# Index queries of a decoder layer: split once where they are turned, kept as stacked high and low parts, and scored in even turns with the value projection

## The chip, the cores and the metric

The kernel runs on one core of a Trainium2 chip. The metric is the device time of one execution in microseconds, the median over several runs. The engines are TensorE (PE, and PEld for its weight loads), VectorE (DVE), ScalarE (ACT), GpSimd (POOL) and SyncE (SP). POOL and SP also issue DMA transfers.

## The reference

One layer of a hybrid decoder for 512 tokens of width 2048. What matters here is the sparse attention group, whose keys are chosen by an indexer of 16 heads of 64:

```python
def block(bargs):
    q_b, qi_b, wi_b, start = bargs
    qpos = start + jnp.arange(Q_BLOCK)
    dots = jnp.einsum('qhi,ki->qhk', qi_b, ki_s, ...) * (IDX_DIM ** -0.5)
    score = jnp.einsum('qh,qhk->qk', wi_b, jax.nn.relu(dots)) * (IDX_HEADS ** -0.5)
    visible = kpos[None, :] <= qpos[:, None]
    score = jnp.where(visible, score, -jnp.inf)
    _, idx = lax.top_k(score, topk)          # topk = 128
    k_sel, v_sel = k_s[idx], v_s[idx]
    logits = jnp.einsum('qhd,qkhd->qhk', q_b, k_sel, ...) * (dh ** -0.5)
    ...
```

`qi` and `ki` are projections of the normed tokens, turned by rotary angles (`rope`). Around it stand the norm and its conditioning by `c`, a stick-breaking attention group of 8 heads, the two gates, the output projection, and a gated MLP with a convolution. Everything is in float32.

## The kernel before

The layer is one program for the core, with tokens along the free dimension (tiles of 128 channels by 512 tokens). A float32 product is made of three matmuls over split operands: each operand is a high part (an ACT copy to the rounded type `fp32r`) and a low part (a DVE subtraction), and `mm3` (L177 to L179) adds high x high, high x low and low x high. Weights stream in on the SP queue as `raw` tiles and are split by `parts`: L167 on ACT writes `wh`, L169 on DVE writes `wl`, into three `rooms` that are used in turn. `split` (L196 and L198) does the same for activations.

The order on each engine is set when the program is built, by a scheduler that takes the code's order as a guide; an engine then runs its instructions strictly in that order. Code in `with behind(x)` is placed after `x`. Side work is written as Python generators, which the main code advances a step at a time.

**The units.** Most projections are done in 31 `unit` calls over `w_x`, each with seven block products on TensorE (a Strassen-like scheme). A unit calls `between` twice, and each call advances the generator `beside`. A part of `beside` is `index_ropes`: for each of eight tiles of index queries (two heads of 64 on 128 partitions) and one tile with the index key, it loads the tile `r` (tag `w`, two buffers), and `rope_steps` turns it: a DVE product (L746), four ACT copies that exchange halves (L749 and L750), then in the next step a DVE product (L752) and sum (L754). Its two temporaries lie in a tile with the tag `soft`, which has one buffer. The turned tile is saved by POOL to DRAM, `td_index[j]` (L786). Only tokens from 128 on (`LATE`, 384 of 512) are needed of the queries. POOL's queue in the units also has the saves of the units' results (`xd`, L882) and the accumulating saves of `mix` (L824).

**The indexer stage.** After the units, `indexer` loads the key and the eight query tiles (`queries`). For each head, `stacked` makes an operand of 128 partitions that holds the high part of the head's 64 channels on one half and their low part on the other (L944 on ACT, L945 on DVE). `score` multiplies it with the key's parts (L954), takes the relu (L956 on ACT, tag `w`) and accumulates with the head's weight on DVE (L959, L960). Scores are made for token blocks 1, 2 and 3 in turn, two heads of one block in a step, so 8 steps for each block. `seen` masks a finished block on POOL (L964), and `chosen` takes the 128 largest by rounds of MAX8 and MATCH_REPLACE8 on DVE (L971, L972); a few of these rounds are placed between the scores.

TensorE's other work in this stage is `values`, a projection (`w_vb`) of 192 matmuls that also is a generator; a step of it is six matmuls. After seven steps at the start, the loop alternates one step of `index` with steps of `fill`: two with each of the eight steps of block 1, and one with every second step after that. Then come the stick-breaking heads: POOL loads `xd` tiles (L892), ACT scales the query (L1055), TensorE makes `heads_z` (L1063), with the next part of the values (`values_narrow`, L1043) as its filling work.

Of the kernel before, what the change touches and what calls it, by code (L numbers as in the profile page):

```python
# [10 lines left out]
F32 = mybir.dt.float32  # L11
F32R = mybir.dt.float32r
BF16 = mybir.dt.bfloat16
I32 = mybir.dt.int32
AF = mybir.ActivationFunctionType
ALU = mybir.AluOpType
PSUM = bass.MemoryType.PSUM

P = 128
D = 2048  # L20
S = 512
# [55 lines left out]
def block_kernel(ctx: ExitStack, tc: tile.TileContext, A: dict, out: bass.AP):  # L77
# [14 lines left out]
    def slot(dt=F32):  # L92

        return t2k("F", SLOTS, dt)
# [99 lines left out]
    def split(src, hi=None, lo=None):  # L194
        hi = slot(F32R) if hi is None else hi
        pins["hi"] = act(hi, src, AF.Copy)  # L196
        lo = slot(F32R) if lo is None else lo
        tt(lo, src, hi.bitcast(F32), ALU.subtract)  # L198
        return hi, lo
# [149 lines left out]
    @contextmanager  # L349
    def behind(*pins):  # L350

        with ExitStack() as stack:
            for p in pins:
                stack.enter_context(tc.issue_after(p.ins))
            yield
# [401 lines left out]
        for _ in rope_steps(src, dst, cosv, sinv, half, n, t2k("ta", 2), t2k("sp", 2)):  # L757
            pass

    td_index = dram("index", 9)  # L760

    def index_ropes():

        tabs = [t2k("T", 2) for _ in range(2)]
        for i, t in enumerate(tabs):
            save(t, rope_d[1][:, i * S : (i + 1) * S])
        def get(j):
            r = t2k("w", 2)
            if j < 8:
                save(r[:, LATE], qid[j][:, LATE])  # L770
            else:
                save(r[:TN], td_tail[:TN])
            return r

        ahead = get(0)
        yield
        for j in range(9):
            r, ahead = ahead, get(j + 1) if j < 8 else None
            soft = sb.tile([P, 10 * P], F32, tag="soft", name=nm("soft"))
            tmp = soft[:, :S], soft[:, S : 2 * S]  # L780
            if j < 8:
                yield from rope_steps(r, [r], *tabs, 32, P, *tmp, LATE)
            else:
                yield from rope_steps(r, [r[:64], r[64:]], *tabs, 32, 64, *tmp)
            at = LATE if j < 8 else slice(0, S)
            save(td_index[j][:, at], r[:, at])  # L786
            yield

    def pause():
# [100 lines left out]
    def fetch(src, rows=slice(0, P)):  # L890
        t = slot()
        save(t[rows], src[rows])  # L892
        return t
# [23 lines left out]


    bias = [causal]

    def queries(j):
        t = slot()
        save(t[:, LATE], td_index[j][:, LATE])
        return t

    def indexer():

        kiR = split(fetch(td_index[8]))
        tail = fetch(td_tail, slice(0, TN))
        raw = [queries(j) for j in range(8)]  # L930
        yield
        wps = outs()
        for b in range(NQB):
# [3 lines left out]
        nc.vector.tensor_copy(wi.rearrange("p b h -> p (b h)"), wps[:, : NQB * IDXH])  # L937
        bias.extend(slot()[:, : (b + 1) * P] for b in range(1, NQB))
        yield

        def stacked(j, a):
            hi, lo = slice(a * IDXD, (a + 1) * IDXD), slice((1 - a) * IDXD, (2 - a) * IDXD)
            both = slot(F32R)
            pins["hi"] = act(both[hi, LATE], raw[j][hi, LATE], AF.Copy)  # L944
            pins["lo"] = tt(both[lo, LATE], raw[j][hi, LATE], both[hi, LATE].bitcast(F32), ALU.subtract)  # L945
            return both

        ops = []

        def score(n, b):  # L950
            W, sc = (b + 1) * P, bias[b]
# [23 lines left out]
            ts(sc, sc, TAKEN, NEG, ALU.not_equal, ALU.mult)  # L975

        for j in range(8):
            ops.extend(stacked(j, a) for a in range(2))
            for a in range(2):
                last = score(2 * j + a, 1)  # L980
            yield last
# [29 lines left out]
    for i in range(24):  # L1011
        run(index)
        if i < 8:
            h[2 * i] = split(halves_[i])
            if i < 6:
                halves_.append(fetch(hd_[i + 2]))
        with behind(pins["dots"], pins["hi"], pins["lo"]):
            run(fill, 2 if i < 8 else 1 - i % 2)
    run(fill, 2)


# [940 lines left out]
```

## Time and profile before

| | us |
|---|---|
| median of 3 runs | 2678.71 (2678.19 to 2680.88) |
| the profiled execution | 2679.04 |
| its span, first to last instruction | 2677.3 |
| TensorE busy | 2645.4 (99%) |
| DVE busy | 2372.4 (89%) |
| ACT busy | 1489.7 (56%) |
| POOL busy | 409.5 (15%) |

The granted TensorE clock is 0.998 over the span. The turns of index queries begin at 394 us and the last of their results is saved at 556 us; the indexer's scores run from 817 to 878 us.

How to read the rows: a timeline row has the start and the length in us, the engine, the line, the operation, what it writes <- what it reads, and in brackets the engine's idle time before it and what ended it. A row of a group has the count (x), the busy time in us, the mean in ns, and the idle time before. PE instructions overlap, so the distance between starts says what one costs. "L12" is line 12 of the kernel.

### The profile page before, as it was taken

To read this page: it belongs to the slowest core of one execution; us is meant where nothing else is said; L and a number is where in the kernel's file an instruction comes from. 1 tells how busy PE (TensorE), PEld (TensorE's weight loads), DVE (VectorE), ACT (ScalarE), POOL (GpSimd) and SP (SyncE) were. 2 spreads that over 40 slices of the span, in tenths; PEclk is the share of its full clock that TensorE was granted. 3 is DMA by queue.
4 is the path that set the end of the run, shared out by engine and by line. 5 is a ranking of instruction groups with operands and counts; after the bars stand their busy time and mean duration, and the time that the engine had idled before them with its cause. 6 is when DMAs were issued, how large, how long until landed. Compare 5 with 4: busy or idle time off the path is not lost.

```text
span 2677.3 us, 48400 instructions
## 1 busy us (share of the span) xinstructions
PE 2645.4 (99%) x18854; PEld 2440.7 (91%) x18854; DVE 2372.4 (89%) x3331; ACT 1489.7 (56%) x2143; POOL 409.5 (15%) x637
## 2 busy tenths in 40 slices
PE   8999999999999999999999999999999999999998
PEld 7779999999997888889999999999999998887876
DVE  9989989999987888889888999999999997888887
ACT  5445455655556776435565556555555555546443
POOL 0011112211122123332220000000000001003121
PEclk9999999999999999999999999999999999999999
DMA  9985768889894349866763457666666647559785
GB/s 362 340 293 186 230 217 241 239 256 275 263 265 162 108 142 327 283 196 201 227 201 104 134 182 192 182 180 181 183 179 182 179 134 244 154 173 243 217 228 158
DMA packets 182038, 564.84 MB, mean 211 GB/s; under 512 B 24868, under 2 KB 26676, under 8 KB 181808
## 3 DMA queue, kind: packets, MB, share of 16 engines
q1 hardware_dynamic: 120976, 399.59, 45.7%
q0 software_dynamic: 60336, 161.71, 23.3%
q8 instruction: 148, 2.42, 0.4%
q14 instruction: 82, 0.67, 0.1%
q10 hardware_dynamic: 496, 0.45, 0.1%
HBM read 451.96 MB, written 106.28 MB: 209 GB/s over the span
## 4 chain that ended last, share of the span: by engine, by line
PE 86%; DVE 4%; DMA 4%; issue 4%; ACT 2%; POOL 1%; ACTq 0%; SPq 0%; DVEq 0%; POOLq 0%
PE att L179 13%; PE att L178 13%; PE att L177 13%; PE acc L178 12%; PE acc L179 12%; PE acc L177 12%; PE att L1043 1%; DVE wl L169 1%; DMA raw<-in_w_qi 1%; DMA sumd<-F 1%; PE outs L178 1%; PE outs L177 1%; PE outs L1224 1%; PE outs L179 1%; PE outs L1111 1%
## 5 line engine op out<-in xcount | busy, mean ns | idle before, releaser
L167 ACT ACTIVATE wh<-raw 128x1024 fp32r<-128x1024 f32 (+2 forms) x783 | 821.6, 1055 | 887.7 <-DVE raw L294 186.5
L169 DVE TENSOR_TENSOR wl<-raw,wh 128x1024 fp32r<-128x1024 f32 (+2 forms) x783 | 944.2, 1213 | 122.8 <-ACT wh L167 116.2
L177 PE MATMUL acc<-F,wh 128*128 128x256 f32 (+3 forms) x2427 | 692.4, 286 | 1.2 <-ACT F L521 1.0
L179 PE MATMUL acc<-F,wl 128*128 128x256 f32 (+3 forms) x2427 | 690.2, 284 | 1.9 <-DVE wl L169 1.9
L178 PE MATMUL acc<-F,wh 128*128 128x256 f32 (+3 forms) x2427 | 689.9, 284 | 0.6 <-DVE F L198 0.3
L177 PE MATMUL att<-F,wh 128*128 128x256 f32 (+2 forms) x2420 | 689.7, 285 | 0.0
L179 PE MATMUL att<-F,wl 128*128 128x256 f32 (+2 forms) x2420 | 687.4, 284 | 0.5 <-DVE wl L169 0.5
L178 PE MATMUL att<-F,wh 128*128 128x256 f32 (+2 forms) x2420 | 686.8, 284 | 0.1
L177 PEld LDWEIGHTS acc<-F,wh 128*128 128x128 f32 (+1 forms) x2427 | 454.7, 187 | 12.8 <-ACT wh L167 3.0
L179 PEld LDWEIGHTS acc<-F,wl 128*128 128x128 f32 (+1 forms) x2427 | 454.9, 187 | 10.1 <-DVE wl L169 3.1
L178 PEld LDWEIGHTS acc<-F,wh 128*128 128x128 f32 (+1 forms) x2427 | 455.0, 187 | 8.7 <-DVE F L549 0.5
L177 PEld LDWEIGHTS att<-F,wh 128*128 128x128 f32 x2420 | 454.3, 188 | 7.6 <-ACT wh L167 1.7
L179 PEld LDWEIGHTS att<-F,wl 128*128 128x128 f32 x2420 | 454.2, 188 | 7.2 <-DVE wl L169 1.5
L178 PEld LDWEIGHTS att<-F,wh 128*128 128x128 f32 x2420 | 454.3, 188 | 6.6 <-DVE F L198 0.9
L178 PE MATMUL att<-wl,F 128*128 128x512 f32 x384 | 150.5, 392 | 0.6 <-DVE wl L169 0.6
L177 PE MATMUL att<-wh,F 128*128 128x512 f32 x384 | 150.3, 392 | 0.2 <-ACT wh L167 0.2
L179 PE MATMUL att<-wh,F 128*128 128x512 f32 x384 | 150.0, 391 | 0.0
L178 PE MATMUL acc<-wl,F 128*128 128x512 f32 x288 | 113.7, 395 | 2.1 <-DVE wl L169 2.0
L177 PE MATMUL acc<-wh,F 128*128 128x512 f32 x288 | 112.8, 393 | 1.4 <-ACT wh L167 1.4
L179 PE MATMUL acc<-wh,F 128*128 128x512 f32 x288 | 111.4, 391 | 0.0
L1423 POOL DMA_DIRECT2D yd<-w x41 | 22.8, 557 | 516.3 <-DVE w L1422 502.8
L332 DVE TENSOR_TENSOR raw<-raw,raw 128x1024 f32<-128x1024 f32 x79 | 96.4, 1220 | 1.3
(439 smaller groups left out, 4106.8 us busy)
## 6 DMA issues: line engine op xcount, KB each, us to landing
raw<-in_w_up SPq DMA_DIRECT2D x164, 512.0 KB, 3.8
raw<-in_w_x SPq DMA_DIRECT2D x128, 512.0 KB, 4.7
raw<-in_w_ada SPq DMA_DIRECT2D x124, 512.0 KB, 5.8
raw<-in_w_down SPq DMA_DIRECT2D x98, 512.0 KB, 4.7
xd<-F POOLq DMA_DIRECT2D x64, 256.0 KB, 4.2
mix<-F POOLq DMA_DIRECT2D x64, 256.0 KB, 6.6
F<-xd POOLq DMA_DIRECT2D x64, 256.0 KB, 5.6
raw<-in_w_o SPq DMA_DIRECT2D x32, 512.0 KB, 4.6
```

The costliest lines, as they stand in the source:

```text
L167: pins["wh"] = act(wh, raw, AF.Copy)
L169: pins["wl"] = tt(wl, raw, wh.bitcast(F32), ALU.subtract)
L177: mm(ps, ah, bh, start=first, stop=False, skip_group_check=not check)
L178: mm(ps, ah, bl, start=False, stop=False, skip_group_check=not check)
L179: return mm(ps, al, bh, start=False, stop=last, skip_group_check=not check)
L332: tt(a12, a12, s, ALU.subtract)
L1043: mm(narrow[b // 2][:, at], x, y, start=i == n == b % 2 == 0, stop=i == KT - 1 and n == 2, skip_group_check=True)
L1111: mm(o[:, kb * P :], vs[kb][:, hd % 4 * HD : (hd % 4 + 1) * HD], w[NQB - 1 - kb], start=i == 0, stop=i == 3, skip_group_check=True)
L1224: mm(o[:, b * P : (b + 1) * P], vs[kb][:, hd % 4 * HD : (hd % 4 + 1) * HD], pT[b][:, kb * P : (kb + 1) * P], start=kb == 0, stop=kb == b)
L1423: nc.gpsimd.dma_start(yd[j // 2][:, j % 2 * S : (j % 2 + 1) * S], a)
```

## The change

The index queries are split in `index_ropes`, right after they are turned: an ACT copy of the whole tile gives the high part and a DVE subtraction the low part, written over the two temporaries in `soft`. Four stores on POOL, each of 64 partitions, put them into DRAM tiles `stacked` of 128 x 512, one for each head, in the layout that `score` needs. The key keeps its store (`td_index`, now one tile). In the indexer `queries(n)` loads a ready operand for each head: eight at the start (`EARLY`), then two with each step of block 1. The sixteen ACT copies and sixteen DVE subtractions of the inner `stacked` are gone. `fill` gets one step with every step of the index loop, and is placed only behind the scores' matmul. The number of value steps is the same.

```diff
-    td_index = dram("index", 9)
+    td_index = dram("index", 1)[0]
+    stacked = [dr.tile([P, S], F32R, tag=f"stacked{n}", name=f"stacked{n}") for n in range(16)]
@@ index_ropes
-            at = LATE if j < 8 else slice(0, S)
-            save(td_index[j][:, at], r[:, at])
+            if j == 8:
+                save(td_index, r)
+            else:
+                hi, lo = (t[:, LATE].bitcast(F32R) for t in tmp)
+                act(hi, r[:, LATE], AF.Copy)
+                tt(lo, r[:, LATE], hi.bitcast(F32), ALU.subtract)
+                for a in range(2):
+                    own, other = slice(a * IDXD, (a + 1) * IDXD), slice((1 - a) * IDXD, (2 - a) * IDXD)
+                    save(stacked[2 * j + a][own, LATE], hi[own])
+                    save(stacked[2 * j + a][other, LATE], lo[own])
@@ the indexer
-    def queries(j):
-        t = slot()
-        save(t[:, LATE], td_index[j][:, LATE])
+    EARLY = 8
+
+    def queries(n):
+        t = slot(F32R)
+        save(t[:, LATE], stacked[n][:, LATE])
         return t
-        kiR = split(fetch(td_index[8]))
+        kiR = split(fetch(td_index))
-        raw = [queries(j) for j in range(8)]
+        ops = [queries(n) for n in range(EARLY)]
-        def stacked(j, a):
-            hi, lo = slice(a * IDXD, (a + 1) * IDXD), slice((1 - a) * IDXD, (2 - a) * IDXD)
-            both = slot(F32R)
-            pins["hi"] = act(both[hi, LATE], raw[j][hi, LATE], AF.Copy)
-            pins["lo"] = tt(both[lo, LATE], raw[j][hi, LATE], both[hi, LATE].bitcast(F32), ALU.subtract)
-            return both
-
-        ops = []
         for j in range(8):
-            ops.extend(stacked(j, a) for a in range(2))
+            ops.extend(queries(n) for n in range(len(ops), min(2 * j + EARLY + 2, 16)))
@@ the loop over index and fill
-        with behind(pins["dots"], pins["hi"], pins["lo"]):
-            run(fill, 2 if i < 8 else 1 - i % 2)
+        with behind(pins["dots"]):
+            run(fill)
```

Three places show how instructions move. The first is DVE at the end of one unit, where a query has been turned and the next is begun. Before (L298 adds a unit's sum, L594 is a step of the conditioning, L280 a sum of weights, L746 begins the next query's turn):

```order
L169 TENSOR_TENSOR wl_69<-raw_4224,wh_66 128x1024
L298 TENSOR_TENSOR sp_4325<-att_4222,ta_4258 128x256
L746 TENSOR_TENSOR soft_4358<-w_4122,T_4058 128x384
L594 SCALAR_TENSOR_TENSOR raw_4289,macc_67<-raw_4289,raw_94 128x1024
L169 TENSOR_TENSOR wl_75<-raw_4230,wh_72 128x1024
L280 TENSOR_TENSOR raw_4494<-raw_4460,raw_4462 128x1024
L169 TENSOR_TENSOR wl_82<-raw_4228,wh_78 128x1024
L752 TENSOR_TENSOR soft_4358<-soft_4358,T_4059 128x384
```

Now (L791 is the new subtraction):

```order
L791 TENSOR_TENSOR soft_4132<-w_4070,soft_4132 128x384
L298 TENSOR_TENSOR sp_4338<-att_4230,ta_4266 128x256
L594 SCALAR_TENSOR_TENSOR raw_4297,macc_67<-raw_4297,raw_94 128x1024
L169 TENSOR_TENSOR wl_75<-raw_4238,wh_72 128x1024
L280 TENSOR_TENSOR raw_4507<-raw_4473,raw_4475 128x1024
L746 TENSOR_TENSOR soft_4371<-w_4130,T_4066 128x384
L169 TENSOR_TENSOR wl_82<-raw_4236,wh_78 128x1024
L752 TENSOR_TENSOR soft_4371<-soft_4371,T_4067 128x384
```

The subtraction of the query turned before stands ahead of L298, and the next query's L746 has moved from behind L298 to behind L280, ahead of a weight split.

The second is POOL between two such queries. Before (L786 saves a turned query, L770 loads the one after next):

```order
L824 DMA mix_1916<-F_4296 128x512
L786 DMA index_1906<-w_4122 128x384
L882 DMA xd_1640<-F_4353 128x512
L770 DMA w_4590<-qid_885 128x384
L882 DMA xd_1641<-F_4354 128x512
L824 DMA mix_1917<-F_4366 128x512
```

Now (L794 and L795 are the new stores of high and low parts; L833, L891 and L771 are the former L824, L882 and L770):

```order
L833 DMA mix_1924<-F_4309 128x512
L891 DMA xd_1640<-F_4366 128x512
L891 DMA xd_1641<-F_4367 128x512
L794 DMA stacked_1908<-soft_4371 64x384
L794 DMA stacked_1909<-soft_4371 64x384
L795 DMA stacked_1908<-soft_4371 64x384
L795 DMA stacked_1909<-soft_4371 64x384
L833 DMA mix_1925<-F_4379 128x512
L771 DMA w_4608<-qid_885 128x384
```

One store has become four, and they stand behind both saves of the unit and ahead of a `mix` save and the next query's load.

The third is POOL at the end of the indexer. Before (L964 masks blocks 1, 2 and 3 as their scores are complete; L892 loads the first heads):

```order
L964 AFFINE_SELECT F_9218<-F_9218 128x128
L964 AFFINE_SELECT F_9219<-F_9219 128x128
L892 DMA F_9826<-xd_1618 128x512
L892 DMA F_9828<-xd_1619 128x512
L892 DMA F_9843<-vd_898 128x512
L892 DMA F_9845<-vd_899 128x512
L892 DMA F_9847<-vd_900 128x512
L892 DMA F_9849<-vd_901 128x512
L892 DMA F_9875<-xd_1620 128x512
L892 DMA F_9877<-xd_1621 128x512
L964 AFFINE_SELECT F_9220<-F_9220 128x128
```

Now:

```order
L965 AFFINE_SELECT F_9266<-F_9266 128x128
L965 AFFINE_SELECT F_9267<-F_9267 128x128
L965 AFFINE_SELECT F_9268<-F_9268 128x128
L901 DMA F_9842<-xd_1618 128x512
L901 DMA F_9844<-xd_1619 128x512
L901 DMA F_9859<-vd_898 128x512
```

The loads of the first heads have moved behind the mask of block 3. On TensorE, 30 matmuls of L1043 now stand ahead of the first `heads_z`, where there were 38.

## The prediction

> **What bounds the kernel now.** I read the page first: busy shares and the chain.
>
> ```profile
> PE 2645.4 (99%) x18854; PEld 2440.7 (91%) x18854; DVE 2372.4 (89%) x3331; ACT 1489.7 (56%) x2143; POOL 409.5 (15%) x637
> PE 86%; DVE 4%; DMA 4%; issue 4%; ACT 2%; POOL 1%; ACTq 0%; SPq 0%; DVEq 0%; POOLq 0%
> ```
>
> TensorE sets the time nearly everywhere, so an edit matters only where it makes TensorE wait or stop waiting. DVE, at 89%, has little air. The change touches two stages, so next I read the stretches: one unit of the projections, in which an index query is turned, and the three parts of the indexer stage.
>
> ```profile
> 413.05:432.09 19.04, 19.04 (x170) 19.04 (x169) 17.33 (x21) 11.57 (x17) 3.96 (x7) 1.00 0.84 244
> 817.30:847.50 30.20, 27.98 (x130) 23.04 (x130) 26.24 (x44) 21.78 (x43) 2.58 (x5) 0.94 0.41 141
> 847.50:864.00 16.50, 15.42 (x68) 11.64 (x68) 14.03 (x36) 9.18 (x18) 0.29 (x1) 1.00 0.21 65
> 864.00:878.30 14.30, 12.98 (x53) 9.24 (x52) 13.19 (x30) 9.32 (x16) 4.73 (x9) 1.00 0.52 184
> ```
>
> Columns are the length, busy PE, PEld, DVE, ACT, POOL, then clock, DMA share and GB/s. The unit is full on TensorE and 17.33 of 19.04 us full on DVE. In the indexer the first part (scores of block 1) contains a TensorE stall at a lower clock, and in the other two DVE is 14.03 of 16.50 and 13.19 of 14.30 us busy while TensorE waits in small pieces.
>
> **Part 1, the indexer: what it gains.** TensorE's rows there:
>
> ```profile
> 820.45 0.39 PE L179 MATMUL att<-wh,F 128*128 128x512 f32 x1
> 822.97 1.09 PE L954 MATMUL acc<-F,F 128*128 128x256 f32 x4 [2.13 <-DVE F L945]
> 823.89 0.41 PE L177 MATMUL att<-wh,F 128*128 128x512 f32 x1
> 828.24 0.64 PE L954 MATMUL acc<-F,F 128*128 128x256 f32 x4
> ...
> 844.34 0.64 PE L954 MATMUL acc<-F,F 128*128 128x256 f32 x4
> 844.81 0.40 PE L177 MATMUL att<-wh,F 128*128 128x512 f32 x1
> 847.56 0.87 PE L954 MATMUL acc<-F,F 128*128 128x384 f32 x4
> 848.27 0.40 PE L177 MATMUL att<-wh,F 128*128 128x512 f32 x1
> ...
> 872.76 1.07 PE L954 MATMUL acc<-F,F 128*128 128x512 f32 x4
> 873.66 0.39 PE L177 MATMUL att<-wh,F 128*128 128x512 f32 x1
> ```
>
> By starts, four score matmuls (L954) take 0.47, 0.71 and 0.90 us for blocks 1, 2 and 3, and twelve value matmuls (two steps) take 2.75 us (844.81 to 847.56), so one step takes 1.375 us. The stall of 2.13 us waits for the split of the stacked queries (L945), and the twelve value matmuls behind it take 4.35 us (823.89 to 828.24), 1.6 more than at full clock. What is removed, and what DVE has beside it:
>
> ```profile
> L945 DVE TENSOR_TENSOR F<-F,F 64x384 fp32r<-64x384 f32 x16 | 8.8, 553 | 4.3 <-ACT F L944 3.8
> L944 ACT ACTIVATE F<-F 64x384 fp32r<-64x384 f32 x16 | 8.3, 517 | 2.9 <-DMA F<-index 2.7
> ACT w L956 <- DVE F L960: 10.0, 22, 1.1
> L960 DVE SCALAR_TENSOR_TENSOR F<-w,wi,F 128x256 f32<-128x256 f32 x15 | 7.2, 483 | 1.4 <-ACT w L956 0.9
> L198 DVE TENSOR_TENSOR F<-F,F 128x512 fp32r<-128x512 f32 x8 | 5.5, 690 | 1.0 <-ACT F L196 0.8
> ```
>
> The first two rows are what goes; the last two are DVE's other work in block 1. The third row is from the waits of 847.5 to 878.4: there the score's relu waits for DVE's accumulation (L960) 22 times, and TensorE for the relu. The even turns put eight value steps (11.0 us of TensorE) out of block 1 and into blocks 2 and 3, where DVE was the pace. TensorE's bare work from the first score to the first matmul of the next values (817.33 to 878.33, 61.0 us): 8 x (0.47 + 0.71 + 0.90) = 16.6, and 150 value matmuls at 0.229 = 34.4, so 51.0; the slack is 10.0. With the new order the parts need 8 x (0.47 + 1.375) = 14.8, then 16.7, 18.2 and a last step of 1.4 on TensorE. DVE needs some 15 of 14.8 in block 1 (16 accumulations at 0.48, eight splits at 0.69 less overlap, two or three weight splits at 1.22), about 15.2 of 16.7 and 17.4 of 18.2 in the others (its busy time there, with one more weight split each and the accumulations that now end after 878.3). TensorE leads, narrowly. I leave 1.5 us of the slack standing for block 1, where loads of `hd` now queue among eight more loads on POOL: **gain 8.5**. Its ends: 10.0 if no wait is left, 3.7 if only the stall and its slow clock go.
>
> A price stands at its end. POOL asks for the first heads only behind the third mask (`seen`), which waits for DVE's last accumulation:
>
> ```profile
> 864.17 0.47 POOL L964 TENSOR_SCALAR_AFFINE_SELECT F<-F 128x128 f32<-128x128 f32 x1 [16.27 <-DVE F L960]
> 864.66 1.09 POOL L892 DMA_DIRECT2D F<-xd  x2
> F<-xd POOLq DMA_DIRECT2D x6, 256.0 KB, 3.1
> 878.33 0.28 PE L1043 MATMUL att<-wh,F 128*128 128x256 f32 x1
> 882.77 0.81 PE L1063 MATMUL acc<-F,F 128*128 128x384 f32 x2
> ```
>
> From the last accumulation, mask and two issues take about 1.1 us and landing 3.1: 4.2. TensorE has, behind its last score, 2.75 us of values and 30 of the 38 matmuls that now take 4.45 us (3.5): 6.25, less 1.4 for the relu and accumulation, so 4.85 against 4.2. Hidden, with 0.65 to spare; beyond it each us is lost. The eight postponed matmuls are only moved.
>
> **Part 2, the units: what it costs.** Each turned query (eight of them, one a unit) gains an ACT copy of 128x384 and a DVE subtraction, and on POOL four half-height stores for one. The DVE subtraction is about 0.55 us (as L754 below) and lies where DVE idles 0.46 us for L298; it costs nothing by itself. ACT is 11.57 of 19.04 busy. POOL gets 24 more stores here and 8 more loads in the indexer at 0.54 us, and is 3.96 of 19.04 busy. But both halves lie in `soft`, which has one buffer: the next query's turn (L746 on DVE, L749 and L750 on ACT) must wait until all four stores have landed. Before, `soft` was free as soon as L754 had read it. One unit, DVE then ACT:
>
> ```profile
> 411.36 1.23 DVE L169 TENSOR_TENSOR wl<-raw,wh 128x1024 fp32r<-128x1024 f32 x1 [0.23 <-ACT wh L167]
> 413.05 0.42 DVE L298 TENSOR_TENSOR sp<-att,ta 128x256 f32<-128x256 f32 x1 [0.46 <-PE att L179]
> ...
> 417.27 1.22 DVE L169 TENSOR_TENSOR wl<-raw,wh 128x1024 fp32r<-128x1024 f32 x1
> 419.21 0.56 DVE L752 TENSOR_TENSOR soft<-soft,T 128x384 f32<-128x384 f32 x1 [0.72 <-ACT soft L750]
> 420.02 0.55 DVE L754 TENSOR_TENSOR w<-soft 128x384 f32<-128x384 f32 x1
> 420.92 1.22 DVE L169 TENSOR_TENSOR wl<-raw,wh 128x1024 fp32r<-128x1024 f32 x1
> ...
> 430.40 1.23 DVE L169 TENSOR_TENSOR wl<-raw,wh 128x1024 fp32r<-128x1024 f32 x1 [0.24 <-ACT wh L167]
> 415.71 1.06 ACT L167 ACTIVATE wh<-raw 128x1024 fp32r<-128x1024 f32 x1 [1.66 <-PE att L178]
> 417.05 0.53 ACT L749 ACTIVATE soft<-w 32x384 f32<-32x384 f32 x1
> 419.21 0.72 ACT L823 ACTIVATE F<-F,c_col 128x512 f32<-128x512 f32 x1
> ```
>
> The subtraction comes at 412.5, after the first L169 here. Then 0.55, a hop of 0.1 to POOL and one issue of 0.55 until the fourth store is issued at 413.7. The price of landing is the unknown. Nearest rows, from the DMA list of 400 to 540 us:
>
> ```profile
> index<-w POOLq DMA_DIRECT2D x8, 192.0 KB, 5.5
> xd<-F POOLq DMA_DIRECT2D x15, 256.0 KB, 4.2
> DMA to landing us min/median/max: 4.7/5.4/6.8
> ```
>
> The last row is of `index` alone. I take T = 5.5, the store that these replace, from the same place in the program: each is half its size, but four go together with a DMA share of 0.84. Bounds 4.2 and 6.8. So `soft` is free at 419.2; ACT's four turns, which began at 417.05 and took 2.16, now begin there; L752 starts at 421.4 instead of 419.21; and in order behind it L330, L754, L331 and the weight split of 420.92, which now ends at 424.3 instead of 422.14. Who waits: the split rooms are three deep, a room came free at 415.7, and TensorE's products take 19.04 / 7 = 2.72, so the product that needs this split starts at 423.8, its low part at 424.05. The slack is 1.9 us: the first time TensorE loses 0.3.
>
> It repeats. From L752 (419.21) to the subtraction behind the last L169 (430.40) DVE has 12.3 us, 11.87 without two small gaps. So the loop from one subtraction to the next is 1.2 + T + 2.16 + 11.87 = 15.2 + T, 20.7 at 5.5 against 19.04 of TensorE: 1.7 us later in each unit. Eight turns wait, the last (the key, two copies for four) shorter by about 0.7: in all 2.16 + 7 x 1.7 - 0.7 - 1.9 = **loss 11.4**. At T = 4.2 it is about 1, at 6.8 about 22; under 3.8 nothing. Beyond the slack every 0.1 us of T is 0.8 us of time.
>
> The Trainium skill (DMA: Bandwidth & Descriptors, Anatomy of one DMA) puts a DMA of this path at 2.0 us plus its bytes at 436 GB/s: an estimate by that page is 2.2 us for a store of 96 KB, under which DVE would not wait and the sum would be 2670.5, rival (b). The trace disagrees: 192 KB would be 2.5 by it, and took 5.5. The same page (Rules for kernel authors) says that two transfers to disjoint partition halves serialize and are better as one; this speaks against the four stores, and no run here shows a half-height one.
>
> **The sum.** The profiled execution took 2679.04 with a span of 2677.3, 0.3 above the median of the runs. 2679.0 - 8.5 + 11.4 = **2682**.
>
> **The rivals.** (a) The stores land late: T of 6 to 6.8, the longest of `index`, makes DVE's wait cost 15 to 22, so 2686 to 2692. For it: DMA is shared with the weight loads at 0.84. Against: 96 KB is less than 192. It is slower beyond 0.2% (5.4 us) from T = 5.8. Chance 0.27. (b) The stores hide: T at 3.8 or less leaves the gain alone, 2670.5, and up to 4.4 the loss is 3 and the change still measurably faster. For it: 256 KB of `xd` in 4.2 in the same stretch. Against: `index` never under 4.7. Chance 0.18. (The 2.0 us and bytes of the Trainium skill, DMA: Bandwidth & Descriptors, Anatomy of one DMA, would give this case.) (c) The even turns don't bring what they say: DVE keeps the pace of blocks 2 and 3, or the heads' loads come later than 4.85 us and TensorE stands before L1063; the gain is the stall's 3.7, less up to 2 there: 2679 + 11.4 - 2.7 = 2688. For it: DVE's 17.4 of 18.2. Chance 0.08. (d) The forecast, within 0.2% (about what a measurement of this kernel can tell from no change) of 2679, at 2682: 0.47.
>
> So faster 0.18, same 0.47, slower 0.27 + 0.08 = 0.35. The forecast's own range is 2674 to 2684. The full one reaches to the gain with a loss of 2 (2672) and to (a) at T = 6.6 (20 - 8.5, 2690).
>
> **What would show it.** In the new profile: no L944 or L945 group, no stall before the second pair of scores and the clock at 1.00 there (part 1); the first matmul of the next values about 8.5 us sooner after the first score; POOL's heads loads behind the mask and no idle before the heads' first matmul. In the units: idle before L746 on DVE and the first L749 on ACT put down to the stores of `stacked`, some 2 us each; units of about 20.7 instead of 19.04 us while queries are turned; TensorE idle before L179 by DVE's `wl`. If units stay at 19.04 us, T or my slack is wrong; if the indexer's stretch does not shrink, the even turns are.

## The result and the profile after

The changed kernel takes 2694.6 us (median of six runs) against 2679.8 of the kernel before in the same session: a ratio of 1.0056, 95% interval 1.0042 to 1.0070, so slower by 11 to 19 us. The prediction was 2682, in a range of 2672 to 2690. The profiled execution took 2695.74 us with a span of 2694.0, against 2679.04 and 2677.3.

The busy times on the page of the changed kernel say little, as they did before; the first row is the engines, the second the chain of what ended last:

```profile
PE 2647.7 (98%) x18854; PEld 2446.4 (91%) x18854; DVE 2366.4 (88%) x3323; ACT 1482.6 (55%) x2135; POOL 426.8 (16%) x669
PE 77%; issue 8%; DMA 6%; DVE 4%; POOL 2%; ACT 2%; ACTq 0%; POOLq 0%; SPq 0%; DVEq 0%
```

TensorE has the same work (2647.7 for 2645.4 us), but its share of the chain is 77% for 86%, and DMA's is 6% for 4%. What it waits for stands in the waits of 390 to 590 us, in which eight queries and the key are turned (engine, line, tile, releaser: sum, times, longest):

```profile
DVE soft L746 <- DMA stacked<-soft: 19.1, 7, 3.4
ACT soft L749 <- DMA stacked<-soft: 17.9, 7, 3.1
```

Seven times both engines stand 2.0 to 3.4 us at the head of a turn until the stores of the turn before it have landed (an eighth wait, 2.8 us at the key, has another releaser's name). The first such unit in the timeline, across engines:

```profile
413.40 0.52 ACT L790 ACTIVATE soft<-w 128x384 fp32r<-128x384 f32 x1
414.21 1.10 POOL L794 DMA_DIRECT2D stacked<-soft  x2 [5.31 <-ACT soft L790]
414.42 0.55 DVE L791 TENSOR_TENSOR soft<-w,soft 128x384 fp32r<-128x384 f32 x1
415.30 1.07 POOL L795 DMA_DIRECT2D stacked<-soft  x2
420.93 0.56 DVE L746 TENSOR_TENSOR soft<-w,T 128x384 f32<-128x384 f32 x1 [2.13 <-DMA stacked<-soft]
423.14 0.56 DVE L752 TENSOR_TENSOR soft<-soft,T 128x384 f32<-128x384 f32 x1 [0.51 <-ACT soft L750]
423.62 0.42 DVE L330 TENSOR_TENSOR sp<-att,ta 128x256 f32<-128x256 f32 x1
424.18 0.36 PE L177 MATMUL att<-F,wh 128*128 128x256 f32 x1 [1.10 <-DVE sp L330]
```

POOL issues the four stores one after the other until 416.4; `soft` comes free at 420.9; the turn's L752 follows at 423.1, and behind it L330, the addition that reads the accumulator `r2`. TensorE's last product of the unit, T4, adds into that accumulator and so waits for L330: 1.10 us idle here, and 1.2 to 2.3 us in each of the next seven units. The lengths of the units from one subtraction L791 to the next (first, fifth and seventh of seven; length, busy PE, PEld, DVE, ACT, POOL, then clock, DMA share, GB/s):

```profile
414.42:434.84 20.42, 19.32 (x171) 19.16 (x170) 17.70 (x24) 11.78 (x18) 5.65 (x10) 1.00 0.82 234
497.45:519.00 21.55, 19.30 (x171) 19.14 (x170) 17.68 (x24) 11.74 (x18) 5.62 (x10) 1.00 0.78 223
539.86:562.81 22.95, 20.78 (x168) 20.61 (x168) 17.89 (x23) 12.89 (x19) 5.42 (x10) 0.93 0.75 211
```

No unit has its 19.04 us; DVE's busy time has hardly moved (17.7 for 17.33), it is idle time that was added. In the last of them TensorE also ran at a lower clock after its wait. In the indexer the two other parts stand, from the first score to the first matmul of the next values:

```profile
836.76:852.66 15.90, 15.22 (x82) 12.96 (x81) 12.54 (x24) 10.50 (x24) 6.95 (x13) 1.00 0.97 319
852.66:869.66 17.00, 16.97 (x81) 14.54 (x80) 15.76 (x37) 9.96 (x19) 0.29 (x1) 1.00 0.27 88
869.66:889.17 19.51, 19.51 (x87) 15.98 (x86) 18.52 (x41) 12.30 (x21) 0.47 (x1) 1.00 0.18 55
```

That is 52.4 us for 61.0, with TensorE busy in 51.7 of them and its clock at 1.00. Right behind it the heads wait:

```profile
885.54 1.07 PE L955 MATMUL acc<-F,F 128*128 128x512 f32 x4
889.17 0.36 PE L1044 MATMUL att<-wh,F 128*128 128x256 f32 x1
889.21 0.74 DVE L961 SCALAR_TENSOR_TENSOR F<-w,wi,F 128x512 f32<-128x512 f32 x1
890.02 0.29 POOL L965 TENSOR_SCALAR_AFFINE_SELECT F<-F 128x128 f32<-128x128 f32 x1 [18.01 <-DVE F L961]
890.50 1.09 POOL L901 DMA_DIRECT2D F<-xd  x2 [0.18 <-issue]
891.57 2.12 POOL L901 DMA_DIRECT2D F<-vd  x4
893.39 0.63 ACT L1056 ACTIVATE F<-F 128x512 f32<-128x512 f32 x1 [1.59 <-DMA F<-xd]
893.68 2.13 POOL L901 DMA_DIRECT2D F<-xd  x4
894.11 0.89 PE L1064 MATMUL acc<-F,F 128*128 128x384 f32 x2 [1.17 <-ACT F L1056]
901.10 0.88 PE L1064 MATMUL att<-F,F 128*128 128x384 f32 x2 [1.45 <-DMA F<-xd]
```

The last accumulation ends at 889.95, the mask follows, and only then POOL asks for the first head, the values and the second head. Both heads stand for their loads. In the kernel before, all eight loads stood behind the second mask, at 864.17, and the third came 17 us after it:

```profile
865.74 2.12 POOL L892 DMA_DIRECT2D F<-vd  x4
867.85 1.07 POOL L892 DMA_DIRECT2D F<-xd  x2
881.45 0.29 POOL L964 TENSOR_SCALAR_AFFINE_SELECT F<-F 128x128 f32<-128x128 f32 x1 [12.53 <-DVE F L960]
```

**Where the time went.** How much later the same matmul starts than before, taken along the program: 1.9 us ahead of the first turn, 18.7 behind the last, 19.4 at the first score, 10.8 at the next values, 13.8 at the second head, 16.7 at the end. So: units +16.8, indexer -8.6, heads +2.95, stretch between units and indexer +0.7; together +11.8. The other 4.9 lie in stages whose instructions are the same. Some 1.5 us of them came at about 160 us and as much at about 2620, each beside a granted clock below 1 (0.75 from 160 to 165 us, 0.83 from 2615 to 2625) that the kernel before did not have there. Such stages vary from one profile to the next: the first turn (L746) starts between 393.7 and 397.1 us in the profiles of this study, with the same work ahead of it.

### The profile page after: what moved, and what is told of

Read it like the earlier page. It is cut to its first block, busy times and chain, and to the rows that moved or that the text cites. A ratio compares the mean times of both kernels' runs of the same rounds, so it can differ in the third digit from the quotient of the medians.

```text
span 2694.0 us, 48470 instructions
## 1 busy us (share of the span) xinstructions
PE 2647.7 (98%) x18854; PEld 2446.4 (91%) x18854; DVE 2366.4 (88%) x3323; ACT 1482.6 (55%) x2135; POOL 426.8 (16%) x669
## 4 chain that ended last, share of the span: by engine, by line
PE 77%; issue 8%; DMA 6%; DVE 4%; POOL 2%; ACT 2%; ACTq 0%; POOLq 0%; SPq 0%; DVEq 0%
PE acc L178 12%; PE acc L179 12%; PE acc L177 12%; PE att L177 11%; PE att L179 11%; PE att L178 11%; DVE wl L169 1%; DMA raw<-in_w_qi 1%; PE outs L178 1%; PE outs L177 1%; PE outs L179 1%; PE att L1044 1%; DMA T<-in_w_va 1%; DMA mix<-F 1%; DMA F<-x1d 0%
## 5 line engine op out<-in xcount | busy, mean ns | idle before, releaser
L179 PEld LDWEIGHTS acc<-F,wl 128*128 128x128 f32 (+1 forms) x2427 | 455.0, 187 | 10.1 <-DVE wl L169 3.1
```

Source lines behind the costliest of these rows:

```text
L179: return mm(ps, al, bh, start=False, stop=last, skip_group_check=not check)
```

## The experiments

The theory from the comparison: the stores hold `soft`, so the next turn waits for their landing, and a loop runs through DVE (subtraction, four issues, landing, turns, the rest of DVE's unit) that is longer than TensorE's unit. The heads lose part of the indexer's gain because the even turns moved their loads behind the third mask. Rivals: the added work itself; the turns or the split alone as the source of the gain; a wait that only T4's position causes.

**1. Room of its own.** The four stores stay; what they read is no longer needed by the next turn.

```
+        soft = sb.tile([P, 10 * P], F32, tag="soft", ...)     # once, ahead of the turns
-            soft = sb.tile([P, 10 * P], F32, tag="soft", ...) # in each turn
-            tmp = soft[:, :S], soft[:, S : 2 * S]
+            tmp = soft[:, :S], soft[:, S - P : 2 * S - P]
-                hi, lo = (t[:, LATE].bitcast(F32R) for t in tmp)
+                hi, lo = soft[:, 7 * P :].bitcast(F32R), r[:, LATE].bitcast(F32R)
```

> The change, but the stores no longer hold the room that the next query's turn needs: `soft` is taken once for all turns, the high part has columns of its own in it, and the low part is written over the turned query, which is not stored any more. The same four half-height stores, the same copy and subtraction, the same loads, the same indexer. Theory (the turn waits for the stores of the turn before it, and TensorE's last product of a unit, T4, waits behind that turn for the addition L330): no idle before L746, no TensorE idle before T4, units of 19.04 us again while queries are turned; the 16.8 us that the units lost are back and the time is 2674 (2679.8 - 8.6 + 2.95, the stages of the indexer and the heads) to 2678 (2694.6 - 16.8). Rival (the added work itself, 24 more stores on POOL and one more instruction each on ACT and DVE per query): the units stay above 20 us and the time above 2690.

Measured: 2676.7 us, ratio to before 0.9985 (0.9976 to 0.9994). A unit, and the wait that took the place of DVE's:

```profile
414.00:433.04 19.04, 19.04 (x170) 19.04 (x169) 17.80 (x23) 11.98 (x17) 5.61 (x10) 1.00 0.90 253
```

```profile
POOL w L771 <- DMA stacked<-w: 24.0, 6, 4.7
```

The units are back at 19.04 us with the same ACT copy, DVE subtraction and 32 stores in them, and TensorE is never idle there. The landing is no shorter; POOL now waits for it, six times 4 us, before it loads the query after next, and no wait of TensorE or DVE in these units is put down to POOL or to these stores. The added work is ruled out: the wait on the room was the loss. This version is faster than both kernels.

**2. The split with the old turns, and the even turns without the split.** Two halves of the change:

```
 # split_only: the change, but
-            run(fill)
+            run(fill, 2 if i < 8 else 1 - i % 2)
 # turns_only: the kernel before, but
-            run(fill, 2 if i < 8 else 1 - i % 2)
+            run(fill)
```

> The change with the old turns of the first values: two value steps for each of the first eight index steps, then one for every second. So the split is in the units, and the indexer has no split, but its old order. Before, 61.0 us lie between the first score and the first matmul of the next values, in the changed kernel 52.4. Theory (part of the gain is the stall on the split and the slow clock behind it, 3.7; the rest is the even turns, for DVE sets the pace of blocks 2 and 3 in the old order): 57.3 us there, units as in the changed kernel, heads' loads not waited for; in all 2679.8 + 16.8 - 3.7 = 2693 to 2696. Rival (the split was the whole of it: DVE without the 8.8 us of L945 no longer sets the pace in either order): 52.4 to 53 us there, 2688 to 2691. Second rival (the even turns are the whole of it): 61 us there, 2697.

> The kernel before, with the even turns alone: one value step behind each index step; the queries are still loaded whole and split in the indexer. Theory (even turns bring 4.9 by themselves, the stall on the split stays): 56 us between the first score and the first matmul of the next values, less up to 2.95 at the heads, units at 19.04 us: 2675 to 2678. Rival (with the split's 8.8 us on DVE still in block 1, which now has half the TensorE work beside it, DVE sets the pace of block 1 as well, and nothing is gained): 61 us there, 2680 to 2683.

Measured: the split alone 2693.8 us (1.0046, 1.0033 to 1.0058), the even turns alone 2686.0 (1.0017, 1.0008 to 1.0026). From the first score, in us:

| kernel | next values | second head's scores | the same matmul behind the second head, against before |
|---|---|---|---|
| before | 61.0 | 70.8 | 0 |
| changed | 52.4 | 64.3 | -5.6 |
| split alone | 56.4 | 66.3 | -4.5 |
| even turns alone | 62.8 | 74.1 | +4.1 |
| own room | 53.2 | 64.6 | -5.4 |

The third column alone can mislead. In the old order 61 matmuls of the next values stand ahead of the second head, with the even turns 53, and each takes 0.12 us, so 0.9 us of the difference is work that comes later. The last column has the same work behind it in every row (it is taken 400 matmuls behind the first score).

For the split alone the theory held (56.4 for 57.3, both rivals out). For the even turns alone it fell, and the rival was right in kind: they lose 1.8 us up to the next values and 4.1 in all by themselves. Their waits from the first score to the next values:

```profile
PEld acc L954 <- DVE F L945: 7.6, 10, 2.8
PE acc L954 <- DVE F L945: 5.6, 6, 2.3
```

With half the value steps beside it, block 1 stops at the split of each operand (L945) and not once. So the two parts are not additive: even turns cost 4.1 with the split in the indexer and, taken from 56.4 to 52.4, bring 4.0 without it, of which the heads' wait leaves 1.1 (-5.6 for -4.5 in the last column).

**3. The heads' loads.** First the first pair alone ahead of the last four index steps:

```
     for i in range(24):
+        if i == 20:
+            pairs = [[fetch(xd[2 * i]), fetch(xd[2 * i + 1])] for i in range(1)]
         run(index)
 ...
-    pairs = [[fetch(xd[2 * i]), fetch(xd[2 * i + 1])] for i in range(1)]
```

> The change, but the first two heads are asked for before the last four index steps and not behind the third mask. Theory (in the changed kernel the heads' first matmul waits 1.17 us and the second head's 1.45 us for loads that POOL issues only behind the mask; with the copy and the pipeline 2.95 us are lost between the next values and the heads): no idle before L1064, 2.95 us less, 2691.6. Rival (the loads are late because the transfer is slow among eight others, not because they are asked for late, or the index steps' DVE work is what the heads wait for next): under 1 us gained, 2694.

Measured: 2696.0 us, 1.0058 (1.0044 to 1.0072): no gain, the rival's number. The first head no longer waits, but the second stands 1.99 us, since its loads still go out behind the mask and the four values; 63.0 us to its scores for 64.3, of which 0.6 is five matmuls of the next values that now come later. So all eight were moved, on top of the room of its own:

> Own room for the stores (2676.7 against 2680.8 before), with even turns, and all eight loads that the first two heads need (the first pair, four of the values, the second pair) asked for ahead of the last four index steps, so ahead of the third mask, as they stood in the kernel before. Theory (the even turns had moved all eight of them behind the third mask; asking for the first pair alone only made the second head wait): 53 us from the first score to the next values as with own room alone, no idle before L1064 or what it is called here, second head's scores 62.2 us or less after the first score instead of 64.6; 2.4 us less, 2674.3. Rival (DVE, not the loads, holds the heads after the even turns): 64 us to the second head's scores, 2676 to 2677.

Measured: 2676.8 us, 0.9983 (0.9974 to 0.9992), and 64.7 us to the second head's scores. The idle at the heads is gone and another has come, in block 3:

```profile
861.48 0.63 ACT L1059 ACTIVATE F<-F 128x512 f32<-128x512 f32 x1 [4.04 <-DMA F<-xd]
862.02 1.06 ACT L957 ACTIVATE w<-acc 128x512 f32<-128x512 f32 x2
862.63 0.75 DVE L961 SCALAR_TENSOR_TENSOR F<-w,wi,F 128x512 f32<-128x512 f32 x1 [3.49 <-ACT w L957]
862.65 0.77 PE L955 MATMUL acc<-F,F 128*128 128x512 f32 x1 [2.33 <-ACT w L957]
```

The copy that scales the first head (L1059) moved up on ACT with its load, and two relus stand behind it while it waits. Holding the copies behind the last relu removes that:

```
-    scaled(0)
+    with behind(pins["relu"]):
+        scaled(0)
 ...
-        with behind(*[last] if before else []):
+        with behind(last if before else pins["relu"]):
             scaled(hd + 1)
```

> The kernel with own room and early loads of the heads, but the copies that scale the first two heads' queries stand behind the last relu of the index steps on ACT. In the run before it, the early loads took the idle time ahead of the heads away, and 64.7 us still lay between the first score and the second head's scores (64.6 with own room alone), because ACT stood 4.0 us at the first copy for its load, with two relus queued behind it, and TensorE 2.3 us for them. Theory (the loads then cost nothing and the wait on ACT is the only thing that took their gain): no idle of TensorE over 1 us from the first score to the second head's scores, 62.2 us there, 2 to 2.5 us less, 2674.4. Rival (DVE's accumulations run that far behind that TensorE waits for DVE whatever the loads do): 64 us or more there, 2677.

Measured: 61.4 us to the second head's scores, 0.59 us the longest idle: in this stretch the theory, also by its number (62.2). The time is 2675.6, 0.9983 (0.9974 to 0.9992), where it said 2674.4: the ratio is the same as without the hold. The 3.2 us against the room of its own are seen in the profile there (3.4 by the same matmul); 1.3 of them are left at the end of the sparse heads (276.4 us after the first score for 277.7), and over the whole the interval cannot tell this version from the room of its own.

**4. The old turns with the room of its own.**

> Own room for the stores and the old turns of the first values (two for each of the first eight index steps, then every second). Theory (with the old turns the split saves 4.5 us in the indexer, as it did with the stores holding `soft`, and the heads' loads stay ahead of the third mask; the even turns add 3.3 to that but lose 2.4 of it again at the heads): 56.5 us from the first score to the next values, second head's scores after 66.3; about 1 us more than with the even turns, 2676.3 to 2678. Rival (the even turns are worth their 4 us once the split is out): 2680.

Measured: 2677.2 us, 0.9984 (0.9975 to 0.9992); 56.5 and 66.3 us. Right by its numbers, but the four versions with own room lie within 1.7 us of each other: once the units are whole, what the even turns add is below what these runs can tell.

**5. Is it the loop, or only T4's place?** L330 is put ahead of the turn's L752. L331, which reads its result, comes ahead of L754 with it; no other order changes in these units but for the key's L754, behind one weight split.

```
+        pins["u3"] = tt(u3, r2, p1, ALU.add)
-        tt(u3, r2, p1, ALU.add)
-            with behind(*pins):
+            with behind(*after, *([pins["u3"]] if u > 1 and not i else [])):
```

> The change with two DVE instructions of each unit exchanged: the addition L330, for which TensorE's product T4 waits, stands ahead of the turn's L752 and not behind it. Theory (the wait for the stores makes a loop through DVE that is longer than TensorE's unit, so a unit takes the loop's time wherever TensorE happens to stand): the idle before T4 falls from 1.1 to about 0.3 us in the first such unit, the following units still take 20.4 us or more and stop at a weight split instead, 1 us less in all, 2693.6. Rival (T4 behind L752 is all that TensorE ever waits for, and DVE's idle time would absorb the rest): units near 19.04 us, 2680.

Measured: 2687.6 us, 1.0023 (1.0012 to 1.0035): 6.4 us more than before in its session, where the change had 14.8. So some 8 us were won, where the theory said 1 and the rival 15. The units lost 10.1 us instead of 16.8. Its second unit:

```profile
438.50 0.56 DVE L746 TENSOR_TENSOR soft<-w,T 128x384 f32<-128x384 f32 x1 [1.72 <-DMA stacked<-soft]
440.11 0.42 DVE L330 TENSOR_TENSOR sp<-acc,ta 128x256 f32<-128x256 f32 x1
440.68 0.36 PE L177 MATMUL acc<-F,wh 128*128 128x256 f32 x1 [0.54 <-DVE sp L330]
440.73 0.56 DVE L752 TENSOR_TENSOR soft<-soft,T 128x384 f32<-128x384 f32 x1 [0.20 <-ACT soft L750]
```

The loop is there all the same. TensorE did not stop at a weight split instead, as the theory had it: all six times that it idled ahead of T4, T4 started 0.15 us after L330 had ended, and L330 still stands behind L746, which waits for the stores. From each subtraction to the next L746 took 6.5, 6.6, 7.0, 7.3, 7.7, 6.9 and 7.5 us in the change, and the units are that plus 13.9, 13.9, 13.9, 13.8, 13.8, 14.0 and 15.4 (the last with the low clock). With L330 ahead it took 6.5, 6.0, 5.5, 6.7, 7.3, 6.4 and 7.4, and the units are that plus 13.8 to 14.0. So the exchange brought three things, together 6.4 of the 6.7 us: 1.0 in the first unit, where TensorE no longer waited, 1.5 for the stretch at low clock that did not come, and 3.9 because `soft` came free 0.56 us sooner on average. The last was not foreseen. The rows of POOL in this second unit show what goes with it:

```profile
431.27 1.08 POOL L794 DMA_DIRECT2D stacked<-soft  x2 [3.67 <-ACT soft L790]
433.33 1.07 POOL L795 DMA_DIRECT2D stacked<-soft  x2 [0.98 <-DVE soft L791]
```

The high part's stores go out 1.2 us ahead of the subtraction, where in the change they went 0.2 ahead and the low part's followed at once. The fourth store then landed after 4.8 us on average in the seven units from the second on, for 5.4 in the change. In the first unit the four went out as in the change, and `soft` came free after 6.5 us as there. That the spacing is the cause was not tried by itself.

**6. Two stores for four.** The same bytes, `soft` held as in the change.

```
 # two_stores: one DRAM tile of 256 rows for both operands of a query
+                save(pairs_d[j].rearrange("(a r) s -> a r s", r=IDXD)[0:4:3, :, LATE], hi)
+                save(pairs_d[j][IDXD : 3 * IDXD, LATE], lo)
 # two_plain: the high parts in one tile, the low parts in another
+                save(stacked[2 * j][:, LATE], hi)
+                save(stacked[2 * j + 1][:, LATE], lo)
```

> The change, but both operands of a pair lie in one DRAM tile, so that the high part goes out as one store of 128 partitions and the low part as another: two stores of 192 KB for four of 96 KB, the same bytes, the room `soft` held as in the change. Theory (the loop from one subtraction to the next is issue + landing + turns + DVE's work; POOL's four issues of 0.54 us end 1.4 us after the subtraction began to be stored, two would end about 0.75 sooner; landing stays 5): units of 20.0 to 20.4 us in place of 20.4 to 21.5, 6 us less, 2688.6. Rival 1 (the landing is a matter of bytes and of a DMA system that is 0.78 busy, not of the count): units as in the change, 2694. Rival 2 (half-height stores are themselves slow, or queue behind each other; the rule of the Trainium skill, DMA: Bandwidth & Descriptors, Rules for kernel authors): landing falls to 4 or less, units at 19.04 to 19.4, 2680 to 2682.

Measured: 2759.8 us, 1.0293 (1.0279 to 1.0307), which no theory had. The DMA of 400 to 590 us, in the change and here, with the stores' rows (count, KB each, median from issue to landing):

```profile
DMA packets 16554, 43.52 MB, mean 229 GB/s; under 512 B 2255, under 2 KB 4303, under 8 KB 16535
stacked<-soft POOLq DMA_DIRECT2D x32, 96.0 KB, 5.5
```

```profile
DMA packets 17225, 31.65 MB, mean 167 GB/s; under 512 B 6848, under 2 KB 8384, under 8 KB 17212
stacked<-soft POOLq DMA_DIRECT2D x13, 192.0 KB, 11.0
```

and, as a row of the stretches, the last 3.5 us before the first such room came free:

```profile
422.00:425.50 3.50, 0.00 (x0) 0.00 (x0) 0.00 (x0) 0.00 (x0) 0.00 (x0) 0.75 0.15 43
```

Three times as many small packets, a landing of 11.0 us, and at its end a DMA share of 0.15 with every compute engine idle. The high part's destination has an outermost dimension of 2. The Trainium skill (DMA: Bandwidth & Descriptors, Rules for kernel authors) says that an outermost dimension below 16 confines a DMA to at most that many of the 16 engines. A share of 0.15 is 2.4 of them, so the trace fits it, though this run shows no share by engine. For the study it was a doubling of the landing: units of 28.7 to 30.3 us between TensorE's waits, 8 longer for a landing 5.5 longer. The question of the count was asked again without that shape:

> The change with two plain stores per query: the high parts of both heads as 128 rows into one DRAM tile, the low parts into another, in rows of 1536 bytes; the indexer puts each operand together with two half-height loads, 32 in all for 16. The room `soft` is held as in the change. So the time of the whole says little, the units say it. In the run with two stores into one shared tile the high part went out in packets under 512 bytes and landed after 11 us instead of 5.5, and units took 29.4 us. Theory (a unit takes the time from the subtraction to the last landing plus 13.9 us, 2.2 of turns and 11.7 of DVE's other work, however many stores there are): units of 13.9 + that time in this run too; with two issues fewer that time is about 0.7 shorter than 7.1 us, so 20.3 us. Rival 1 (the number of transfers delays the landing: two of 192 KB land as `index` did, or sooner): 5.5 us or less, units of 19.4 or less. Rival 2 (a store of 192 KB lands later than one of 96 KB by as much as the issues save): 7 us and units of 21 us as in the change.

Measured, in the units: 25.2, 21.8, 26.0, 25.4 and so on; from subtraction to L746 7.2 to 9.5 us, 8.2 on average over seven units, against 7.1 with four stores. None of the numbers came; rival 2 is nearest: these two stores of 192 KB land later (6.4 us median from issue) than four of 96 KB. The store's row, and two units:

```profile
stacked<-soft POOLq DMA_DIRECT2D x16, 192.0 KB, 6.4
```

```profile
414.16:439.32 25.16, 22.14 (x170) 21.97 (x169) 17.80 (x24) 11.85 (x18) 4.51 (x8) 0.86 0.66 193
439.32:461.11 21.79, 19.30 (x170) 19.13 (x169) 17.59 (x23) 11.83 (x18) 4.50 (x8) 1.00 0.75 218
```

The unit at full clock is 7.4 + 14.4, the loop again; the others are up to 3 us longer, at a clock of 0.86 to 0.93, in which DVE waits for TensorE as well. The time of the whole, 2729.4 (1.0177), also has the doubled loads in it. The Trainium skill's rule that two transfers to partition halves are better as one (same page and section), which the prediction weighed, is not borne out for this landing: 7.1 us with halves, 8.2 with wholes. But it is not refuted either, since on POOL a store of `mix` came to stand between the two. The high part's store, ahead of it, landed 5.3 to 6.4 us after its issue (median 5.8), the low part's, behind it, 4.7 to 8.3 (median 6.9); and in the kernel before, the stores of `index`, also 192 KB, took 4.7 to 5.9. So what the count does by itself stays open.

## Why the prediction was wrong

Two steps failed: the heads' loads, counted as hidden, cost 2.95 us, and the loss in the units, put at 11.4, was 16.8.

**The indexer (part 1)** was right: gain 8.5 forecast, 8.6 measured; blocks of 14.8, 16.7 and 19.6 us forecast (the last with its last step), 15.9, 17.0 and 19.5 measured. The stall and its low clock are gone, and the 1.5 us left standing lie in block 1. What the prediction could not say is how the two parts divide: 4.5 for the split, -4.1 for the even turns by themselves, and the rest only together.

**The heads' loads** failed: "Hidden, with 0.65 to spare" became 2.95 us lost. Two steps were off. The row at 864.17 is the second mask, not the third; in the kernel before, the loads did not depend on the last accumulation at all, and the change moved all eight behind it. And 1.4 us was given to relu and accumulation behind the last score; the score began at 885.54, and the last accumulation ended 4.4 later, since DVE puts a step of the search for the chosen keys between two accumulations. The scaling copy of 0.63 us and the second head's loads behind four others were not in the sum. This is rival (c)'s second half ("TensorE stands before L1063"), at 2.95 for its 2.

**The units (part 2)** had the right mechanism and were too cheap: 11.4 forecast, 16.8 measured. Step by step, the times of the change less its 1.9:
- The fourth store's issue was put at 413.7 and ended at 414.45: "a hop of 0.1 to POOL and one issue of 0.55" left out that the low part's two stores queue behind the high part's. The landing after the end of that issue was 4.6 and not 5.5 (4.6 to 5.6 over the eight). The rows of landing count from the start of an issue, so the sum had counted the issue of 0.55 twice; as the rows count, the fourth store took 5.1 (5.0 to 5.9). By luck the two errors cancel: `soft` free at 419.0 for 419.2, L752 at 421.2 for 421.4.
- "Who waits" named the wrong product. It went past L330 in DVE's row and counted a slack of 1.9 to the weight split behind L331; TensorE already needed L330, for T4. The first unit lost 1.26 us for 0.3. Experiment 5 moved that addition, and in the first unit TensorE no longer waited.
- The loop, "15.2 + T", held to 0.1 us: from the release of `soft` to the next subtraction 13.9 for the 14.0 that it implies. The landing did not hold still: from subtraction to release 6.5 to 7.7, 7.1 on average, for the 6.7 assumed, 2.7 us over seven units, of which the slightly shorter rest of the loop gave back about 1.
- A stretch at low clock after one wait (1.5) and a last turn that was no shorter (0.7) were missed.

**The sum** with the measured terms is 2679.0 - 8.6 + 16.8 + 2.95 + 0.7 = 2690.9: 11.8 more than before, inside the measured interval of 11 to 19. The 3.7 us from there to the median of 2694.6 lie in stages for which the prediction had no term. Rival (a), slower by stores that land late, had the sign but not the cause: its T was 6 to 6.8, and T was hardly longer than forecast in any unit. The 6.8 was a misreading besides: the prediction's row of landings of `index` also holds the indexer's loads, two of which took 6.8; the eight stores that the change replaces took 4.7 to 5.9. Rival (b) did not come: the change's stores landed 5.0 to 6.7 us after their issue, 5.5 in the median, at a DMA share of about 0.8. The Trainium skill (DMA: Bandwidth & Descriptors, Anatomy of one DMA) gives 2.2 us by its fit for such a store, an estimate. One store of experiment 5 landed that soon, where the median was 4.6; no run here shows such a store with the DMA otherwise idle.

## What to carry to other kernels

A store holds the buffer that it reads until it has landed; when that buffer is a single room that the next round writes first, count the loop from issue to landing to the next issue, and compare it with the period of the bounding engine, before asking whether any engine has air. The cure here was a place for the stored data that the next round needs last (the turned query itself); two larger stores, in the two forms tried, made the units longer. When an edit moves steps of one chain, look at what else stood at a fixed place among them on every queue: eight loads changed sides of a mask that nobody had touched.

## What was not expected of the hardware

TensorE ran at about half rate for a while after some of its short waits. In the change, the seventh wait (2.17 us idle) was followed by 16 matmuls at 0.213 us each, 3.4 us, instead of 0.113; the fifth (2.25 us) was not. With two plain stores seven of the eight waits, of 2.29 to 4.60 us, were followed by 14 to 27 such matmuls; one of 2.49 us was not. The Trainium skill (TensorE: Matmul & The Clock Gate, What's actually happening) describes a clock halved after an idle window of about 3.4 us, with windows that run free of the kernel; the 3.4 us at half rate agree, but idles of 2.2 us were enough at times here. A longer one did not always do it: with the split alone the wait of 3.57 us at 549.7 us was followed by matmuls at the full rate.

The two plain stores of 192 KB landed 6.4 us from issue, the four of 96 KB 5.5, both with other transfers beside them and the former with a `mix` store between them. And the price of a wait changed with its place: with one DVE addition exchanged, the same four stores were spaced otherwise, and `soft` came free 0.56 us sooner on average.
